# First stage of a one-core decoder step: the first conditioning result moved ahead of the weight roundings, low parts and scaled blocks moved behind pair 0, parameter transposes behind pair 1, and a pool that waits tile by tile

## Chip, cores and metric

The kernel runs on 1 core of one Trainium2 chip. The metric is device microseconds (us) of one execution. TensorE (PE) has two clock levels, 1.2 and 2.4 GHz; the profile writes the granted one as 0.5 or 1.0 of full speed.

## The reference

One inference step of a one-layer hybrid decoder: 512 prompt tokens and 8 sample tokens of width 1024, all float32. What matters for this change is the start of the layer:

```
cs = silu(c)                                  # c: 9 rows of 1024 (1 prompt, 8 samples)
mod = cs @ w_mod + b_mod                      # 1024 x 6144
sh1, sc1, g1, sh2, sc2, g2 = split(mod, 6)
h = rmsnorm(x, norm1_g) * (1 + sc1) + sh1     # 520 x 1024
u = h @ w_in                                  # 1024 x 8192: columns of q, f, i, gate, ...
f, k, q from sigmoids of u; HGRN2 recurrence with 8 heads; RG-LRU branch; merge; MLP
```

## The kernel before

Every large product is made three times on PE with rounded operands: a matrix is split into a high part (`whi`, `h_hi`, rounded by a ScalarE copy to the fp32r type) and a low part (`wlo`, `h_lo`, the difference, made by VectorE), and `products` adds high·high, high·low and low·high: 6 matmuls of 260 columns for one block of 128 rows of one weight tile. Activations lie transposed, as 8 blocks k of 128 features by 520 tokens.

The code is recorded in program order and a list scheduler places it on the engines; `behind(a, b)` is an ordering hint that forces a after b on an engine without a wait of its own. Each engine runs its list in order. SyncE (SP) issues nearly all loads.

The first stage (`begin`) does this. x is loaded, squared (ScalarE) for the norm, and transposed by PE into `self.x[k]` (tiles `ma`). `normed` broadcasts the factor of the norm and multiplies it into all 8 blocks on VectorE: u = x·rs, L477, tile `xn`. Meanwhile SP loads the conditioning weights `wm` (8 tiles of 1 MB, two for each pair of blocks: part 0 is the shift, part 1 the scale) and the first two tiles of w_in (`wst`, 0.5 MB each, the f and q columns of head 0), in the order wm, wm, wst, wm, wst, and then the other five wm. `first_w` splits these two (L1507 on ScalarE, L1508 on VectorE).

Then a loop runs over four pairs of blocks, k = 0, 2, 4, 6 (pairs 0 to 3 here):

- `mod(k)`: 16 matmuls of the program (32 in the trace) of `wm` against the conditioning rows (L382), and one ScalarE copy of the result out of PSUM (tile `modev`, L385);
- 6 matmuls (`products`) of the pair before;
- `mod_close`: four PE transposes of `modev` (L397), and on VectorE two reductions (L402), the bias (L405) and the gain (L409), which give scale and shift (`modT`);
- the other 18 matmuls of the pair before;
- `affine_split(k)`: h = u·scale + shift for the pair: high parts on ScalarE (L490, the samples' by L494), the full value on VectorE (L486 and L487 for samples, L495), the low part on VectorE (L496).

The products of pair 3 come last, and with them two PSUM accumulators (tile `mm`) are done: f and q of head 0. `parameters_in` transposes small parameters on PE (L242) and copies them out on VectorE (L243). Then the pool `start` is closed and the pool `hg` opened on its memory, and head 0 begins: three sigmoids on ScalarE (L157) read the two accumulators, and the next matmul group (the gate columns) needs the first accumulator's place. `head_sample` scales the sample states on ScalarE (L573) and adds to them on VectorE (L574), from `vb`, a broadcast that goes out to DRAM and back (L564, L566).

Of the kernel before, what the change touches and what calls it, by code (L numbers as in the profile page):

```python
# [6 lines left out]
F32 = mybir.dt.float32  # L7
# [9 lines left out]
L = 512  # L17
# [34 lines left out]
class Kernel:  # L52
# [321 lines left out]
    def mod(self, ws, ev, place):  # L374

        nc = self.nc
        ps = self.pps.tile([128, 512], F32, name="ps")
        for j, w in enumerate(ws):
            n = w.shape[2]
            for k in range(KO):  # L380
                r = 32 * (k % 4)
                ins = nc.tensor.matmul(ps[r:r + 32, j * n:j * n + n], self.cT[:, k, :], w[:, k, :], start=k < 4, stop=k >= KO - 4)  # L382
                if self.ppt_free:
                    self.turn = self.behind(ins, self.turn) if self.turn else ins
        ins = nc.scalar.copy(ev, ps)  # L385
        if self.ppt_free and self.last_hi:
            self.behind(ins, self.last_hi)
        self.mod_open = ev, place
# [76 lines left out]
    def normed(self):  # L465
# [9 lines left out]
        nc.vector.tensor_copy(rsb[:, L:], p2[:, :NB])  # L475
        for k in range(KO):
            nc.vector.tensor_tensor(self.u[:, k], self.x[k], rsb, OP.mult)  # L477

    def affine_split(self, k0):
# [6 lines left out]
        nc.vector.tensor_tensor(f[:, :, L:], u[:, ks, L:T], sc[:, :, 1:9], OP.mult)  # L486
        nc.vector.tensor_tensor(f[:, :, L:], f[:, :, L:], sh[:, :, 1:9], OP.add)  # L487
        for j in range(2):
# [4 lines left out]
            else:  # L493
                self.last_hi = self.behind(nc.scalar.copy(self.h_hi[:, ks, L:T], f[:, :, L:]), ins)  # L494
            nc.vector.tensor_scalar(f[:, j, :L], u[:, k, :L], sc[:, j, 0:1], sh[:, j, 0:1], OP.mult, OP.add)  # L495
            last = nc.vector.tensor_tensor(self.h_lo[:, k, :T], f[:, j], self.h_hi[:, k, :T].bitcast(F32), OP.subtract)  # L496
# [73 lines left out]
    def head_sample(self, h, st, vb, fkq, after):  # L570
        nc = self.nc
        for b in range(NB):
            nc.scalar.activation(st[:, b], st[:, b], AF.Copy, scale=fkq[:, 0, b:b + 1])  # L573
            after = self.behind(nc.vector.scalar_tensor_tensor(st[:, b], vb[:, b], fkq[:, 1, b:b + 1], st[:, b], OP.mult, OP.add), after)  # L574
# [11 lines left out]
    def head_prompt(self, h, f, X, q, v, og, st, vb, fkq):  # L586
# [5 lines left out]
        vn = self.slot(self.hg, "g")  # L592
        nc.scalar.copy(vn[:, :L], pv)

# [885 lines left out]

    def open_pool(self, name, bufs):
        self.scope = ExitStack()
        return self.scope.enter_context(self.tc.tile_pool(name=name, bufs=bufs))

# [3 lines left out]
    def begin(self):  # L1488
# [15 lines left out]

        def first_w(st):
            hi, lo = (self.start.tile([128, KO, 128], F32R, name=n, bufs=2) for n in ("whi", "wlo"))
            self.behind(nc.scalar.copy(hi, st), ready)  # L1507
            nc.vector.tensor_tensor(lo, st, hi.bitcast(F32), OP.subtract)  # L1508
            return hi, lo
# [18 lines left out]
        ready = nc.scalar.activation(self.act0, self.act0, AF.Sigmoid)  # L1528
        self.behind(self.behind(ready, squares), self.exps)
        first = [first_w(st) for st in staged]  # L1530
        par = self.parameters()
# [9 lines left out]
        for k in range(0, KO, 2):  # L1541
            mod(k)
            products(todo[:1])
            self.turn = self.mod_close(self.turn)
            products(todo[1:])
            self.split_last = self.affine_split(k)
            todo = [(j, k + n) for n in (0, 1) for j in (0, 1)]
        products(sorted(todo))
        self.parameters_in(*par)
        self.decays()  # L1550
        self.first = acc
        self.close_pool()
        self.hg = self.open_pool("hg", 2)
        self.ppt_free = False
# [62 lines left out]
```

## Time and profile before

| | |
|---|---|
| median of 3 runs | 1012.51 us (1012.02 to 1013.14) |
| the profiled execution's own time | 1012.61 us |
| its span (first to last instruction) | 1010.8 us |
| PE busy in the span | 981.9 us (97%) |
| VectorE (DVE) busy | 695.4 us (69%) |
| ScalarE (ACT) busy | 516.2 us (51%) |

The span is 1.8 us shorter than the time of the same execution, and that execution lies 0.1 us above the median. Busy time is an average over stages; what a change in one stage is worth is read from the waits of that stage.

### The profile page before, as it was taken

Reading aid. Unit: us, or ns where it says so; the run is one execution under the profiler, and the core shown is the slowest. Engines: PE = TensorE matmul, PEld = TensorE weight load, DVE = VectorE, ACT = ScalarE, POOL = GpSimd, SP = SyncE. Lnnn points to the kernel's source line nnn. Section 1 sums busy time; section 2 is a strip of 40 time slices with the busy share of each in tenths; the row PEclk is TensorE's granted clock in tenths of the full one; section 3 lists DMA queues with packets and bytes.
Section 4 is the critical chain, followed back from the end, with each engine's and each line's share of the span. In section 5 each row is a group of like instructions: output and inputs, shape, how many; then the busy total and the mean of one; then the engine's idle time right before and its main releaser. Section 6 shows DMA issues by size and latency. Waiting matters only on the chain.

```text
span 1010.8 us, 23254 instructions
## 1 busy us (share of the span) xinstructions
PE 981.9 (97%) x9585; PEld 955.3 (95%) x9585; DVE 695.4 (69%) x1543; ACT 516.2 (51%) x985; POOL 106.7 (11%) x193
## 2 busy tenths in 40 slices
PE   4999999999999999999999999999999999999995
PEld 3799999999999999999989999999999999999994
DVE  6768888698879868463233348767767766768775
ACT  5444763574575456351222234466556545646653
POOL 3000000000000000120000000022321331242040
PEclk9899999999999999999999999999999999999998
DMA  9794444353443434586566756222852582282242
GB/s 300 213 263 136 124 129 138 94 161 119 116 136 107 134 96 126 195 268 206 169 188 222 232 166 174 84 84 54 179 146 82 103 194 81 70 183 62 68 79 85
DMA packets 212572, 145.78 MB, mean 144 GB/s; under 512 B 6262, under 2 KB 196878, under 8 KB 212458
## 3 DMA queue, kind: packets, MB, share of 16 engines
q1 hardware_dynamic: 202562, 132.37, 44.1%
q0 software_dynamic: 9904, 11.92, 6.3%
q8 instruction: 75, 1.23, 0.5%
q14 instruction: 31, 0.25, 0.1%
HBM read 123.61 MB, written 13.39 MB: 136 GB/s over the span
## 4 chain that ended last, share of the span: by engine, by line
PE 90%; DVE 4%; DMA 3%; ACT 1%; issue 1%; SPq 0%; DVEq 0%; ACTq 0%; POOLq 0%
PE mm L118 65%; PE ps L1151 8%; PE pt L1151 4%; PE ps L382 2%; PE pb L1151 2%; PE pb L779 1%; PE ps L628 1%; DMA xn<-in_x_prompt_dram 1%; PE mm L1151 1%; PE pt L704 1%; PE pt L717 1%; DVE wlo L87 1%; DMA wst<-in_w_in_dram 1%; DMA vb<-vd 1%; PE pt L628 1%
## 5 line engine op out<-in xcount | busy, mean ns | idle before, releaser
L118 PE MATMUL mm<-h,whi 128*128 128x260 f32 (+1 forms) x3072 | 508.0, 285 | 1.9 <-ACT X L157 1.2
L118 PEld LDWEIGHTS mm<-h,whi 128*128 128x128 f32 x3072 | 425.9, 189 | 6.5 <-ACT whi L84 1.7
L118 PE MATMUL mm<-h,wlo 128*128 128x260 f32 (+1 forms) x1536 | 314.6, 284 | 0.0
L84 ACT CAST whi<-wst 128x1024 fp32r<-128x1024 f32 x166 | 173.9, 1050 | 208.8 <-PE mm L118 171.3
L87 DVE TENSOR_TENSOR wlo<-wst,whi 128x1024 fp32r<-128x1024 f32 x166 | 202.8, 1222 | 88.5 <-ACT whi L84 87.3
L118 PEld LDWEIGHTS mm<-h,wlo 128*128 128x128 f32 x1536 | 239.6, 189 | 0.1
L118 PE MATMUL mm<-a,whi 128*128 128x260 f32 x512 | 82.8, 283 | 0.0
L118 PEld LDWEIGHTS mm<-a,whi 128*128 128x128 f32 x512 | 70.3, 188 | 0.9 <-issue 0.8
L118 PE MATMUL mm<-a,wlo 128*128 128x260 f32 x256 | 51.7, 284 | 0.0
L1247 DVE TENSOR_TENSOR f<-f 128x260 f32<-128x260 f32 x64 | 27.3, 427 | 29.0 <-ACT f L1242 28.3
L880 POOL DMA_DIRECT2D t<-oaT_d x8 | 4.3, 551 | 375.8 <-PE mm L118 368.8
L1236 ACT ACTIVATE ft<-ft,fsh 128x512 f32<-128x512 f32 (+2 forms) x36 | 24.1, 676 | 35.9 <-DVE ft L1233 35.9
L118 PE MATMUL mm<-b,whi 128*128 128x260 f32 x256 | 41.6, 284 | 0.0
L1239 POOL TENSOR_TENSOR ft<-ft,fsh 128x8 f32<-128x8 f32 x28 | 18.5, 659 | 215.7 <-DVE ft L1233 215.7
L118 PEld LDWEIGHTS mm<-a,wlo 128*128 128x128 f32 x256 | 39.4, 188 | 0.0
L118 PEld LDWEIGHTS mm<-b,whi 128*128 128x128 f32 x256 | 35.0, 188 | 2.5 <-issue 2.5
L614 DVE TENSOR_TENSOR Y<-Y,tb 128x512 f32<-128x512 f32 x40 | 27.5, 688 | 11.0 <-ACT Y L616 5.5
L896 DVE TENSOR_TENSOR t<-mm,t 128x520 f32<-128x520 f32 x8 | 5.6, 699 | 37.0 <-PE mm L118 37.0
L1281 POOL DMA_DIRECT2D ma<-snap x28 | 26.1, 933 | 39.4 <-issue 22.1
L1263 POOL DMA_DIRECT2D ma<-snap x28 | 26.1, 932 | 39.7 <-DMA ma<-snap 23.2
L1242 ACT ACTIVATE f<-ft 128x520 f32<-128x520 f32 (+1 forms) x36 | 20.8, 589 | 14.9 <-POOL ft L1240 12.9
L573 ACT ACTIVATE st<-st,fkq 128x128 f32<-128x128 f32 x64 | 19.6, 390 | 13.9 <-DVE fkq L553 12.7
(488 smaller groups left out, 1816.6 us busy)
## 6 DMA issues: line engine op xcount, KB each, us to landing
wst<-in_w_in_dram SPq DMA_DIRECT2D x64, 512.0 KB
wm<-in_w_mod_dram SPq DMA_DIRECT2D x8, 2048.0 KB
wst<-in_w_ff_dram SPq DMA_DIRECT2D x64, 256.0 KB
wst<-in_w_ff_dram SPq DMA_DIRECT2D x32, 512.0 KB
wm<-in_w_mod_dram SPq DMA_DIRECT2D x8, 1024.0 KB
st<-in_state_hgrn_dram SPq DMA_DIRECT2D x8, 512.0 KB
vb<-vd SPq DMA_DIRECT2D x8, 512.0 KB
out_dram<-st SPq DMA_DIRECT2D x8, 512.0 KB
```

The lines of the kernel that those rows point to most:

```text
L84: ins = self.nc.scalar.copy(hi, st)
L87: ins = self.nc.vector.tensor_tensor(lo, st, hi.bitcast(F32), OP.subtract)
L118: self.last_product = self.nc.tensor.matmul(ps[:, s, :c.stop - c.start], x, y[:, c], start=first and n == 0, stop=last and n == 2)
L382: ins = nc.tensor.matmul(ps[r:r + 32, j * n:j * n + n], self.cT[:, k, :], w[:, k, :], start=k < 4, stop=k >= KO - 4)
L614: made = nc.vector.tensor_tensor(view(Y, b, 0, 2 * b, n, b), view(X, b, 0, 2 * b, n, b), fac, OP.mult)
L628: ins = nc.tensor.matmul(*args, start=True, stop=True)
L1151: ins = self.nc.tensor.matmul(ps, x[:, w], y[:, f], start=j in (1, 7, 2) and k == 0 and n == 0, stop=k == 3 and n == 2, skip_group_check=True)
L1236: nc.scalar.activation(t[:, :p], t[:, :p], AF.Relu, bias=sh[:, 0:1])
L1242: nc.scalar.activation(f, self.two(self.ft)[:, a:a + n], AF.Square)
L1247: self.nc.vector.tensor_tensor(f[:, n], f[:, a], f[:, b], op)
L1263: nc.gpsimd.dma_start(x[1][:, b], v[:, :n], accum_op=OP.add)
L1281: nc.gpsimd.dma_start(x[t][:, a], s[p], accum_op=OP.add)
```

## The change

Nothing is computed differently; instructions are put in another order, and waits are cut.

1. The copy of pair 0's conditioning result out of PSUM goes ahead of the two weight roundings (`first_w`) on ScalarE; the first rounding comes right behind it, the second behind pair 0's high parts.
2. On VectorE only the first two scaled blocks (`scaled(0)`, `scaled(1)`) come ahead of pair 0; the low parts of the two weights and blocks 2 and 3 come behind pair 0, blocks 4 to 7 behind pair 1.
3. In `affine_split` each full value (now L500) goes after the low part before it, so that the two blocks of a pair alternate.
4. `parameters_in` is called behind pair 1 instead of after the last products.
5. The pool `hg` is opened with `reuse_waits="tile"`: a tile in it waits for what lay in its own place, not for all of the closed pool.
6. ScalarE's scaling of the sample states is ordered behind the copy of the transposed values (`vcopy`).

```diff
--- before.py
+++ after.py
@@ -382,8 +382,8 @@
                 ins = nc.tensor.matmul(ps[r:r + 32, j * n:j * n + n], self.cT[:, k, :], w[:, k, :], start=k < 4, stop=k >= KO - 4)
                 if self.ppt_free:
                     self.turn = self.behind(ins, self.turn) if self.turn else ins
-        ins = nc.scalar.copy(ev, ps)
-        if self.ppt_free and self.last_hi:
+        self.evicted = ins = nc.scalar.copy(ev, ps)
+        if self.ppt_free:
             self.behind(ins, self.last_hi)
         self.mod_open = ev, place
 
@@ -473,8 +473,12 @@
         rsb = self.c128[:, :T]
         nc.scalar.copy(rsb[:, :L], ps)
         nc.vector.tensor_copy(rsb[:, L:], p2[:, :NB])
-        for k in range(KO):
-            nc.vector.tensor_tensor(self.u[:, k], self.x[k], rsb, OP.mult)
+
+        def scaled(k):
+            ins = nc.vector.tensor_tensor(self.u[:, k], self.x[k], rsb, OP.mult)
+            if self.split_last:
+                self.behind(ins, self.split_last)
+        self.scaled = scaled
 
     def affine_split(self, k0):
 
@@ -484,7 +488,8 @@
         sc, sh = (self.modT[:, p * 8 + k0:p * 8 + k0 + 2] for p in (1, 0))
         u = self.u
         nc.vector.tensor_tensor(f[:, :, L:], u[:, ks, L:T], sc[:, :, 1:9], OP.mult)
-        nc.vector.tensor_tensor(f[:, :, L:], f[:, :, L:], sh[:, :, 1:9], OP.add)
+        sample = nc.vector.tensor_tensor(f[:, :, L:], f[:, :, L:], sh[:, :, 1:9], OP.add)
+        last = None
         for j in range(2):
             k = k0 + j
             ins = nc.scalar.activation(self.h_hi[:, k, :L], u[:, k, :L], AF.Identity, bias=sh[:, j, 0:1], scale=sc[:, j, 0:1])
@@ -492,7 +497,8 @@
                 self.behind(ins, self.last_hi)
             else:
                 self.last_hi = self.behind(nc.scalar.copy(self.h_hi[:, ks, L:T], f[:, :, L:]), ins)
-            nc.vector.tensor_scalar(f[:, j, :L], u[:, k, :L], sc[:, j, 0:1], sh[:, j, 0:1], OP.mult, OP.add)
+            mid = nc.vector.tensor_scalar(f[:, j, :L], u[:, k, :L], sc[:, j, 0:1], sh[:, j, 0:1], OP.mult, OP.add)
+            self.behind(mid, last or sample)
             last = nc.vector.tensor_tensor(self.h_lo[:, k, :T], f[:, j], self.h_hi[:, k, :T].bitcast(F32), OP.subtract)
         self.last_hi = ins
         return last
@@ -570,7 +576,7 @@
     def head_sample(self, h, st, vb, fkq, after):
         nc = self.nc
         for b in range(NB):
-            nc.scalar.activation(st[:, b], st[:, b], AF.Copy, scale=fkq[:, 0, b:b + 1])
+            self.behind(nc.scalar.activation(st[:, b], st[:, b], AF.Copy, scale=fkq[:, 0, b:b + 1]), self.vcopy)
             after = self.behind(nc.vector.scalar_tensor_tensor(st[:, b], vb[:, b], fkq[:, 1, b:b + 1], st[:, b], OP.mult, OP.add), after)
         nc.sync.dma_start(self.o["hgrn_s"][0, :, h].rearrange("b k v -> k b v"), st)
         return after
@@ -590,7 +596,7 @@
         for c in range(NC):
             nc.tensor.transpose(pv[:, c * C:(c + 1) * C], v[:, c * C:(c + 1) * C], self.ident)
         vn = self.slot(self.hg, "g")
-        nc.scalar.copy(vn[:, :L], pv)
+        self.vcopy = nc.scalar.copy(vn[:, :L], pv)
 
 
 
@@ -1478,9 +1484,9 @@
         for _, fn, *a in steps:
             fn(*a)
 
-    def open_pool(self, name, bufs):
+    def open_pool(self, name, bufs, **kw):
         self.scope = ExitStack()
-        return self.scope.enter_context(self.tc.tile_pool(name=name, bufs=bufs))
+        return self.scope.enter_context(self.tc.tile_pool(name=name, bufs=bufs, **kw))
 
     def close_pool(self):
         self.scope.close()
@@ -1502,10 +1508,10 @@
         def mod(k):
             self.mod([raw.pop((part, k)) for part in (0, 1)], self.sm.tile([128, 512], F32, name="modev", bufs=1), (0, 2, k, 2))
 
-        def first_w(st):
+        def first_w(st, after):
             hi, lo = (self.start.tile([128, KO, 128], F32R, name=n, bufs=2) for n in ("whi", "wlo"))
-            self.behind(nc.scalar.copy(hi, st), ready)
-            nc.vector.tensor_tensor(lo, st, hi.bitcast(F32), OP.subtract)
+            self.behind(nc.scalar.copy(hi, st), after)
+            self.split_last = self.behind(nc.vector.tensor_tensor(lo, st, hi.bitcast(F32), OP.subtract), self.split_last)
             return hi, lo
 
         pm, pl = self.parameters_mod(), self.parameters_bounds()
@@ -1526,8 +1532,10 @@
         self.parameters_mod_in(pm)
         self.normed()
         ready = nc.scalar.activation(self.act0, self.act0, AF.Sigmoid)
-        self.behind(self.behind(ready, squares), self.exps)
-        first = [first_w(st) for st in staged]
+        self.last_hi = self.behind(self.behind(ready, squares), self.exps)
+        self.scaled(0)
+        self.scaled(1)
+        first = []
         par = self.parameters()
         acc = [self.pmm.tile([128, 2, 512], F32, name="mm") for _ in range(2)]
 
@@ -1544,13 +1552,20 @@
             self.turn = self.mod_close(self.turn)
             products(todo[1:])
             self.split_last = self.affine_split(k)
+            if k == 0:
+                first += first_w(staged[0], self.evicted), first_w(staged[1], self.last_hi)
+                for n in (2, 3):
+                    self.scaled(n)
+            if k == 2:
+                for n in range(4, KO):
+                    self.scaled(n)
+                self.parameters_in(*par)
             todo = [(j, k + n) for n in (0, 1) for j in (0, 1)]
         products(sorted(todo))
-        self.parameters_in(*par)
         self.decays()
         self.first = acc
         self.close_pool()
-        self.hg = self.open_pool("hg", 2)
+        self.hg = self.open_pool("hg", 2, reuse_waits="tile")
         self.ppt_free = False
         self.fkq = [self.hg.tile([128, 3, 32], F32, name=f"fkq{n}", bufs=1) for n in range(2)]
         for t in self.fkq:
```

The scheduler makes of it the following. On ScalarE, at the start of the loop (`whi` are the roundings of first_w, `modev` the conditioning result, `h` the high parts), before:

```order
L1528 ACTIVATE act0_103<-act0_103 1x1
L1507 CAST whi_340<-wst_187 128x1024
L1507 CAST whi_344<-wst_191 128x1024
L385 COPY modev_360<-ps_361 128x512
L490 ACTIVATE h_151<-xn_160,modT_182 128x512
L494 CAST h_151<-ht_388 128x2x8
L490 ACTIVATE h_151<-xn_160,modT_182 128x512
L385 COPY modev_398<-ps_399 128x512
```

and in the changed kernel:

```order
L1534 ACTIVATE act0_103<-act0_103 1x1
L385 COPY modev_346<-ps_347 128x512
L1513 CAST whi_384<-wst_187 128x1024
L495 ACTIVATE h_151<-xn_160,modT_182 128x512
L499 CAST h_151<-ht_374 128x2x8
L495 ACTIVATE h_151<-xn_160,modT_182 128x512
L1513 CAST whi_388<-wst_191 128x1024
L385 COPY modev_394<-ps_395 128x512
```

The first `modev` has moved ahead of both roundings, and the second rounding behind the high parts of pair 0.

On PE, between pair 0's last products and the products that follow the third conditioning matmuls, before:

```order
L118 MATMUL mm_359<-h_151,wlo_345 128x260 x2
L382 MATMUL ps_461<-wm_197,cT_176 32x256 [waits DMAHW6_49]
L382 MATMUL ps_461<-wm_197,cT_176 32x256 x7
L382 MATMUL ps_461<-wm_195,cT_176 32x256 [waits DMAHW5_49]
L382 MATMUL ps_461<-wm_195,cT_176 32x256 x7
L118 MATMUL mm_358<-h_151,whi_340 128x260 [waits Activation_49] x2
```

and now (`rb`, `rc`, `rd` are the rows of the small parameters; DMAHW and DMASW are semaphores of loads, and a name with _49 one of an engine):

```order
L118 MATMUL mm_345<-h_151,wlo_389 128x260 x2
L242 MATMUL ps_463<-ident_111,rb_334 128x57 [waits DMASW6_49,DMASW5_49,DMASW7_49,DMASW1_49,DMASW0_49]
L242 MATMUL ps_466<-ident_111,rc_335 128x64 [waits DMASW2_49,PE_49]
L242 MATMUL ps_469<-ident_111,rd_336 128x96 [waits DMASW3_49,DVE_49]
L242 MATMUL ps_472<-ident_111,rd_336 128x96 [waits DVE_49]
L382 MATMUL ps_476<-wm_197,cT_176 32x256 [waits DMAHW6_49,DVE_49]
L382 MATMUL ps_476<-wm_197,cT_176 32x256 x7
```

Four transposes stand ahead of pair 2's conditioning matmuls, which now wait for VectorE as well: these tiles `ps` share two PSUM places, so that the place of `ps_476` is free only after the copy out of `ps_469`.

On VectorE, from pair 1's reduction to pair 2's, before:

```order
L402 TENSOR_REDUCE modT_182<-pt_423 128x18 x2
L405 TENSOR_TENSOR modT_182<-modT_182,pm_316 128x2x18
L409 TENSOR_TENSOR modT_182<-modT_182,pm_316 128x18
L486 TENSOR_TENSOR ht_450<-xn_160,modT_182 128x2x8
L495 TENSOR_SCALAR ht_450<-xn_160,modT_182 128x512 x2
L487 TENSOR_TENSOR ht_450<-ht_450,modT_182 128x2x8
L496 TENSOR_TENSOR h_152<-ht_450,h_151 128x520 x2
L402 TENSOR_REDUCE modT_182<-pt_485 128x18 x2
```

and now, from the samples' part of pair 1 on:

```order
L490 TENSOR_TENSOR ht_446<-xn_160,modT_182 128x2x8
L243 COPY pa_460<-ps_463 128x57
L243 COPY pb_461<-ps_466 128x64
L491 TENSOR_TENSOR ht_446<-ht_446,modT_182 128x2x8
L500 TENSOR_SCALAR ht_446<-xn_160,modT_182 128x512
L243 COPY pc_462<-ps_469 128x96
L243 COPY pc_462<-ps_472 128x96
L502 TENSOR_TENSOR h_152<-ht_446,h_151 128x520
L500 TENSOR_SCALAR ht_446<-xn_160,modT_182 128x512
L502 TENSOR_TENSOR h_152<-ht_446,h_151 128x520
L478 TENSOR_TENSOR xn_160<-ma_231,c9_106 128x520
...
L402 TENSOR_REDUCE modT_182<-pt_500 128x18 x2
```

The four parameter copies stand inside pair 1's affine, and four scaled blocks (one shown) between it and pair 2's reduction.

On SP the load of the seventh w_in tile goes ahead of the eight stores of x (`xT_d`), where before it stood behind them.

## Rows read from the trace of the kernel before

**Rows 1.** What PE waited for over the whole span: total us, times, longest.
```profile
PE pt L397 <- ACT modev L385: 4.6, 1, 4.6
...
PE mm L118 <- ACT X L157: 1.2, 1, 1.2
...
PE mm L118 <- DVE h L496: 0.6, 1, 0.6
...
PE pb L779 <- ACT xcs L183: 0.5, 1, 0.5
```
**Rows 2.** Two stretches: engines' busy us, granted clock, DMA share, GB/s.
```profile
20.00:24.00 4.00, 1.44 (x28) 0.61 (x20) 4.00 (x9) 2.56 (x5) 0.00 (x0) 0.98 1.14 321
24.00:30.50 6.50, 4.08 (x33) 2.30 (x36) 6.18 (x18) 3.27 (x5) 0.00 (x0) 0.50 1.09 348
```
**Rows 3.** Timeline, 19 to 31 us: start, duration, instruction, idle before and its releaser.
```profile
19.50 1.93 PE L382 MATMUL ps<-wm,cT 128*32 128x256 f32 x32
...
19.79 0.16 DVE L475 COPY c<-ps 128x8 f32<-128x8 f32 x1
...
24.41 1.05 ACT L1507 CAST whi<-wst 128x1024 fp32r<-128x1024 f32 x1 [1.83 <-DMA wst<-in_w_in_dram]
...
25.36 0.58 ACT L385 COPY modev<-ps 128x512 f32<-128x512 f32 x1
...
25.99 1.11 PE L397 MATMUL pt<-ident,modev 128*128 128x128 f32 x4 [4.55 <-ACT modev L385]
...
27.53 3.46 PE L382 MATMUL ps<-wm,cT 128*32 128x256 f32 x32 [0.42 <-DVE wlo L1508]
```
**Rows 4.** SP's queue: one issue group of the conditioning weights.
```profile
17.72 12.88 SPq L371 DMA_DIRECT2D wm<-in_w_mod_dram  x5
```
**Rows 5.** Timeline of pair 1 and the start of pair 3, 32 to 40 us.
```profile
32.45 0.37 DVE L402 TENSOR_REDUCE modT<-pt 128x18 f32<-128x72 f32 x2 [1.37 <-PE pt L397]
...
33.30 0.82 ACT L490 ACTIVATE h<-xn,modT 128x512 fp32r<-128x512 f32 x1 [1.60 <-DVE modT L409]
...
34.49 1.93 PE L382 MATMUL ps<-wm,cT 128*32 128x256 f32 x32
...
34.50 0.21 ACT L494 CAST h<-ht 128x16 fp32r<-128x16 f32 x1 [0.39 <-DVE ht L487]
...
34.74 1.42 DVE L496 TENSOR_TENSOR h<-ht,h 128x520 fp32r<-128x520 f32 x2 [0.27 <-ACT h L494]
...
37.19 0.66 PE L397 MATMUL pt<-ident,modev 128*128 128x128 f32 x4
...
39.95 1.93 PE L382 MATMUL ps<-wm,cT 128*32 128x256 f32 x32
```
**Rows 6.** Groups of VectorE instructions, 0 to 52 us: count, busy us, mean ns.
```profile
L477 DVE TENSOR_TENSOR xn<-ma,c 128x520 f32<-128x520 f32 x8 | 5.0, 689 | 0.0
L495 DVE TENSOR_SCALAR ht<-xn,modT 128x512 f32<-128x512 f32 x8 | 4.0, 542 | 0.0
...
L1508 DVE TENSOR_TENSOR wlo<-wst,whi 128x1024 fp32r<-128x1024 f32 x2 | 2.4, 1221 | 0.0
```
**Rows 7.** Timeline, 46 to 52 us: parameter copies, last products, first sigmoids.
```profile
46.27 0.42 DVE L243 COPY pc<-ps 128x96 f32<-128x96 f32 x2 [0.21 <-PE ps L242]
...
47.35 0.51 PE L118 MATMUL mm<-h,whi 128*128 128x260 f32 x2 [0.62 <-DVE h L496]
...
50.33 0.60 ACT L157 ACTIVATE e<-mm 128x520 f32<-128x520 f32 x1 [1.44 <-PE mm L118]
...
51.48 0.74 PE L118 MATMUL mm<-h,whi 128*128 128x260 f32 x4 [1.24 <-ACT X L157]
```
**Rows 8.** Timeline of head 0, 67 to 77 us: a late weight, a broadcast.
```profile
67.89 1.05 ACT L84 CAST whi<-wst 128x1024 fp32r<-128x1024 f32 x1 [3.98 <-DMA wst<-in_w_in_dram]
...
70.70 1.25 SPq L566 DMA_DIRECT2D vb<-vd  x1
...
76.86 0.62 DVE L574 SCALAR_TENSOR_TENSOR st<-vb,fkq,st 128x128 f32<-128x128 f32 x2 [2.65 <-DMA vb<-vd]
```

## Prediction

> **What bounds the kernel now.** PE is busy 97% of the span, so time can only be won where PE waits. The list of PE's waits comes first: 4.6 us for the first conditioning result, 1.2 us for a sigmoid, 0.6 us for a low part, 0.5 us in head 0 [rows 1]. Everything but the last lies before 52 us, where this change works. Its ceiling is therefore a few microseconds of 1012.
>
> Next the timeline of the first wait [rows 3]. The conditioning matmuls of pair 0 (I call them mod 0, and so on) end at 19.50 + 1.93 = 21.43 us. Their copy out of PSUM starts at 25.36, because two roundings stand ahead of it on ScalarE, and the second began only at 24.41, when its weight landed. The transposes follow at 25.99, and mod 2 (pair 1) at 27.53.
>
> The reader should look closely at that 27.53. The row names a VectorE instruction as the releaser, but the PSUM place that mod 2 needs was last read by the copy at 19.79 [rows 3], long done. What is left of its waits is its weight. This can be checked: the w_in tile that was awaited landed at 24.41 at the latest, the next in SP's queue is the first of the last five conditioning weights [rows 4], 1.05 MB, and the stretch moved 348 GB/s with the DMA engines full [rows 2]: 24.4 + 3.0 = 27.4 us. So the loads, not the late copy, set the start of mod 2. By the same rate the pairs of weights for mod 4 and mod 6 are complete 6.0 us apart, at 33.4 and 39.4; they started at 34.49 and 39.95 [rows 5], so there PE was the later one, by 1.1 and 0.5 us.
>
> **The change, step by step.** Durations are those of the profiled execution.
>
> *First result ahead.* The copy can start at 21.7, the transposes at 22.3, and at the full-rate price of 0.66 us [rows 5] they end near 23.0 instead of 27.1. That is 4.1 us earlier for scale and shift. PE gains 0.1: its next instruction is mod 2, at 27.4 by the loads. The wait does not go away; it becomes a wait for a transfer.
>
> *The clock.* PE stood still for 4.55 us before [rows 3], and its clock was granted at 0.98 and then 0.50 (the lower level, 1.2 GHz) in the two stretches around it [rows 2]; mod 2 took 3.46 us where a full-rate one takes 1.93. Now PE stands still from 23.0 to 27.4, 4.4 us, nearly as long, so I take the same 3.46 us. No row shows this exact pattern, so it is bounded: if the clock stayed up, mod 2 would be 1.5 us shorter; if the half-rate time began with PE's stop, 1.5 us later than before, and ended as much later, 1.5 us of products would take double, costing 0.75.
>
> The Trainium skill, "TensorE: Matmul & The Clock Gate", in Part 1 on the clock gate, says that the gate's observation is free-running and not tied to the kernel's start, so that the point of change differs from run to run. By that rule the term could fall on either side in any one execution; a single profile, as here, cannot show it.
>
> *Low parts, scaled blocks, second rounding.* They move into 23 to 31 us, where PE waits and then runs mod 2. On VectorE pair 0's scale and shift are ready at 23.9 (0.85 us after the reduction starts, as 32.45 to 33.30 [rows 5]), its low parts at 26.8 (3.7 us after, as 32.45 to 36.16), two weight low parts of 1.22 us at 29.2, two scaled blocks of 0.65 us from start to start (5.0 us for eight) at 30.6 [rows 6]. Mod 2 ends at 30.9. So this costs nothing; without that cover it would cost up to 3.7 us.
>
> *Alternating order in the affine.* The first low part comes earlier by one 0.54 us operation [rows 6], the second at the same time: nothing on the path by itself.
>
> *Parameters behind pair 1.* Here the change adds a wait. Pair 0's products end at 34.4. Then four transposes, of which the third and fourth need VectorE to have copied out the first two. VectorE copies the first at 34.7 (0.2 us each, half of the 0.42 in [rows 7]), the second by 35.15; then in its queue stand a sample operation (0.2) and a full value (0.54), then the third copy, done at 36.0. Mod 4 needs that PSUM place: it starts at 36.05 instead of 34.49, 1.55 us later. In return the old place gives back its transposes and the 0.6 us wait near 47 us, both worked into the following.
>
> *Four scaled blocks behind pair 1.* Queued behind that third copy are the fourth, two low parts and a full value (38.05), and four scaled blocks at 0.65: 40.65. Pair 2's reduction stands behind them. Its transposes are done at 36.05 + 2.70 + 0.66 = 39.4 (37.19 − 34.49 = 2.70 [rows 5]), so it is 1.2 us late. Mod 6 runs at 36.05 + 5.46 = 41.5 (39.95 − 34.49 [rows 5]), its weight long there; pair 2's low parts are done at 40.65 + 3.7 = 44.35, just before their second use. Pair 3's reduction starts at 41.5 + 2.7 + 0.7 = 44.9, its low parts end at 47.8 and 48.6. PE arrives there at 41.5 + 5.46 = 46.95 and must wait for both. After the second, 16 matmuls remain at 0.12 us (18 and four transposes took 39.95 − 37.19 [rows 5]): 50.5, against 50.25 before. So up to here nothing is won: the 0.1 and the 0.6 us are spent.
>
> *Separate waits.* Before, the first sigmoid began at 50.33, with ScalarE idle for 1.44 us, and PE waited 1.24 us until 51.48 [rows 7]. The first accumulator was complete earlier, 12 matmuls or 1.45 us before the end, but the sigmoid's tile waited for all of the closed pool. Now it can begin when ScalarE is free and the accumulator done (49.1 to 49.5); two sigmoids of 0.5 to 0.6 us end at 50.6. The gate matmuls start at 50.65: **0.8 us** earlier than 51.48.
>
> *Later.* In head 0 a weight landed late (ScalarE idle 3.98 us), the broadcast was issued at 70.70 behind it, and VectorE waited 2.65 us for it [rows 8]; PE's 0.5 us [rows 1] follows from that chain. That weight's load now goes ahead of eight stores, so I take this **0.5 us** as won; bounds 0 and 0.5. Scaling the sample states later costs nothing while the broadcast lands after it: 2.5 us of room [rows 8]. Other stalls in the reordered heads can come or go; by the size of [rows 1], 0.5 us either way.
>
> Sum: 0.8 + 0.5 = 1.3 us. From the profiled 1012.6 that gives 1011.3, from the median of the runs shown 1012.5 − 1.3 = **1011.2 us**.
>
> **Rivals.** *(a) The clock stays up, or mod 2 is not held by its load: faster.* For it: the transposes are nearer to mod 0. Against it: the idle time is nearly unchanged. With mod 2 at 1.93 us all starts up to mod 6 move by 1.5 (34.5 and 40.0, still after their loads), 1012.5 − 2.8 = 1009.7. If mod 2 were free of its load, the next loads (33.4, 39.4) still hold: mod 6 at 39.4 instead of 41.5 gives 1009.1.
>
> *(b) It does nothing measurable.* The sigmoid's gain goes into waits for pair 3's low parts, and head 0 keeps its 0.5: 1012.0 to 1012.8. For it: PE's chain is already paced by loads and products.
>
> *(c) Slower: VectorE's queue.* The parameter copies and scaled blocks delay pair 2's reduction to 40.65. The slack behind it is 0.5 us; beyond, each microsecond passes to the end of pair 3. From a reduction at 42.0 on the stage is slower than before; at 43.5, were the copies and blocks as slow as twice their rows, the time would be 1014.0. Against it: these are durations of like instructions.
>
> **How the numbers follow.** Forecast 0.60, (a) 0.20, (b) 0.14, (c) 0.06. 0.2%, about what a measurement of this kernel can tell from no change, is 2.0 us: below 1010.5 is faster, above 1014.5 slower. (a) lies mostly beyond, and the forecast's edge adds a little: faster 0.20, same 0.77, slower 0.03. Range for 8 in 10: from between the two cases of (a), 1009.3, to 1013.0, which takes in (b) and the 0.75 us of the clock.
>
> **What would show it.** First `modev` copy near 21.7; PE idle to 27.4 and then released by a load (another name there is chance); half clock in mod 2; mod 4 at 36; a wait of PE for a low part near 47 to 49; first sigmoid near 49.5 and no wait of 1.2 us at 50; `vb` issued before 70. It is wrong if mod 2 starts well before 27, if it takes 1.9 us, or if mod 4 starts before 35.5.

## The result, and the profile after

The changed kernel took **1014.7 us** (median of 9 runs, 1013.62 to 1016.59) beside 1012.51 us for the kernel before, a ratio of 1.0021 with an interval of 1.0012 to 1.0030: it became slower by 0.2%, clear of the scatter. I had forecast 1011.2 us (1009.3 to 1013.0): the time lies outside the range, on the wrong side. The profiled execution (1015.5 us, 0.8 above the median) has a span of 1013.7 us, 2.9 more than before; the medians lie 2.2 us apart.

PE's waits of after, same view as [rows 1]: total us, times, longest.

```profile
PE ps L382 <- DMA wm<-in_w_mod_dram: 5.5, 1, 5.5
...
PE mm L118 <- DVE e L549: 1.8, 1, 1.8
PE pb L785 <- ACT xcs L183: 1.5, 1, 1.5
...
PE pt L710 <- ACT g L703: 0.8, 1, 0.8
```

The wait for the first conditioning result has become one for a load, as predicted, and the 1.2 us for a sigmoid is gone. But there are three waits behind 52 us, 4.1 us in all: for the product L549 of head 0's output gate (65 us), for `xcs` (88 us; the rounded input of the RG-LRU branch, whose products go to `pb`), and in the products of keys and values of the second head (L710, 140 us). Before there were 0.5 (`pb`, 85 us) and 0.4 (`pt`, 393 us).

PE in the first stage, timeline, to be read beside [rows 3, 5].

```profile
21.34 0.66 PE L397 MATMUL pt<-ident,modev 128*128 128x128 f32 x4 [0.72 <-ACT modev L385]
27.50 3.64 PE L382 MATMUL ps<-wm,cT 128*32 128x256 f32 x32 [5.50 <-DMA wm<-in_w_mod_dram]
31.07 1.24 PE L118 MATMUL mm<-h,whi 128*128 128x260 f32 x4
32.10 0.64 PE L118 MATMUL mm<-h,wlo 128*128 128x260 f32 x2
32.53 0.86 PE L397 MATMUL pt<-ident,modev 128*128 128x128 f32 x4
33.15 0.73 PE L118 MATMUL mm<-h,whi 128*128 128x260 f32 x4
...
36.90 1.93 PE L382 MATMUL ps<-wm,cT 128*32 128x256 f32 x32 [0.40 <-DVE pc L243]
```

Mod 2 is released by its load at 27.50. The half rate, over by mod 2's end before, now covers four products as well (1.24 us, then 0.73), the next two (0.64, elsewhere 0.40) and the transposes. The granted clock says the same; first after, then before (stretch, us, PE busy and count, clock, DMA share, GB/s).

```profile
24.00:27.00 3.00, 0.00 (x0) 0.87 1.09 348
...
30.50:34.00 3.50, 3.50 (x25) 0.63 1.09 347
```

```profile
24.00:27.00 3.00, 1.01 (x4) 0.50 1.09 349
...
30.50:34.00 3.50, 3.50 (x33) 0.98 1.09 347
```

The clock fell later in PE's idle time and rose later in the products: less of the half rate was spent idle.

The end of the stage and head 0, timeline of after (ScalarE, PE, VectorE; to be read beside [rows 7]).

```profile
50.38 0.61 ACT L157 ACTIVATE e<-mm 128x520 f32<-128x520 f32 x1 [0.29 <-ACT whi L84]
...
51.58 0.72 PE L118 MATMUL mm<-h,whi 128*128 128x260 f32 x4
...
60.13 0.30 ACT L770 CAST bdhlru_wa<-bdst 128x128 fp32r<-128x128 f32 x1 [4.10 <-DMA bdst<-in_lru_wa_dram]
...
62.03 0.61 ACT L157 ACTIVATE e<-mm 128x520 f32<-128x520 f32 x1
...
64.22 0.75 DVE L549 SCALAR_TENSOR_TENSOR e<-mm,pa,e 128x520 f32<-128x520 f32 x1
...
65.12 0.72 PE L118 MATMUL mm<-h,whi 128*128 128x260 f32 x4 [1.79 <-DVE e L549]
```

The gate matmuls start at 51.58 without a wait, against 51.48 [rows 7]: the stage has gained nothing. Then head 0 loses. Its output gate (sigmoid at 62.03, product L549 at 64.22) frees the accumulator that PE needs from 63.3 on. Ahead of that sigmoid in ScalarE's queue stand the roundings of the first block weights (`bdst`, the small matrices of the RG-LRU branch), and they waited 4.10 us for a load. In the kernel before the product ended just before PE came to it:

```profile
62.17 0.75 DVE L543 SCALAR_TENSOR_TENSOR e<-mm,pa,e 128x520 f32<-128x520 f32 x1
...
63.12 0.66 PE L118 MATMUL mm<-h,whi 128*128 128x260 f32 x4
```

The second loss, ScalarE and VectorE, 69 to 77 us, and PE at 88.

```profile
69.66 0.30 ACT L770 CAST bdhlru_wa<-bdst 128x128 fp32r<-128x128 f32 x1 [4.26 <-DMA bdst<-in_lru_wa_dram]
71.60 0.30 ACT L770 CAST bdhlru_wx<-bdst 128x128 fp32r<-128x128 f32 x1 [1.65 <-DMA bdst<-in_lru_wx_dram]
71.81 0.58 ACT L599 COPY g<-ps 128x512 f32<-128x512 f32 x1
72.29 2.45 ACT L579 ACTIVATE st<-st,fkq 128x128 f32<-128x128 f32 x8
74.64 1.04 ACT L84 CAST whi<-wst 128x1024 fp32r<-128x1024 f32 x1
...
75.71 1.23 DVE L87 TENSOR_TENSOR wlo<-wst,whi 128x1024 fp32r<-128x1024 f32 x1 [2.09 <-ACT whi L84]
...
87.93 0.39 PE L785 MATMUL pb<-xcs,bdhlru_wa 128*128 128x260 f32 x1 [1.49 <-ACT xcs L183]
```

The second block weights come late; behind them on ScalarE stands the value copy (L599), behind that, by the change's order, the state scaling (2.45 us), and behind that the rounding for which VectorE idles 2.09 us. Everything later in VectorE's queue slips, up to `xcs`. Before, the scaling lay in a wait of ScalarE long ahead of that, and the same rounding came at 70.79:

```profile
55.75 2.46 ACT L573 ACTIVATE st<-st,fkq 128x128 f32<-128x128 f32 x8 [1.19 <-DMA st<-in_state_hgrn_dram]
...
70.79 1.06 ACT L84 CAST whi<-wst 128x1024 fp32r<-128x1024 f32 x1 [0.96 <-PE mm L118]
```

Why the second block weights are late: SP's queue of after and then of before.

```profile
53.30 1.52 SPq L767 DMA_DIRECT2D bdst<-in_lru_wa_dram  x1
...
57.31 0.38 SPq L75 DMA_DIRECT2D wst<-in_w_in_dram  x1
57.74 6.79 SPq L545 DMA_DIRECT2D xT_d<-ma  x8
64.62 0.59 SPq L767 DMA_DIRECT2D bdst<-in_lru_wa_dram  x1
```

```profile
50.74 1.03 SPq L761 DMA_DIRECT2D bdst<-in_lru_wa_dram  x1
...
54.33 6.50 SPq L539 DMA_DIRECT2D xT_d<-ma  x8
61.23 0.38 SPq L75 DMA_DIRECT2D wst<-in_w_in_dram  x1
61.92 0.54 SPq L761 DMA_DIRECT2D bdst<-in_lru_wa_dram  x1
```

The seventh weight's load is not issued before 57.31, when VectorE has made the low part of the fifth weight, whose place it takes (57.29), the eight stores of x stand behind it, and the second block weights behind these: 64.62 instead of 61.92. The first block weight goes out 2.6 us later too, behind one weight more.

### The profile page after: what moved, and what is told of

Read it like the earlier page. It is cut to its first block, busy times and chain, and to the rows that moved or that the text cites. A ratio compares the mean times of both kernels' runs of the same rounds, so it can differ in the third digit from the quotient of the medians.

```text
span 1013.7 us, 23250 instructions
## 1 busy us (share of the span) xinstructions
PE 981.7 (97%) x9585; PEld 955.2 (94%) x9585; DVE 693.3 (68%) x1543; ACT 513.8 (51%) x985; POOL 106.7 (11%) x193
## 4 chain that ended last, share of the span: by engine, by line
PE 89%; DVE 3%; ACT 3%; DMA 2%; SPq 2%; issue 1%; DVEq 0%; ACTq 0%
PE mm L118 64%; PE ps L1157 8%; PE pt L1157 4%; PE ps L382 2%; PE pb L1157 2%; PE ps L634 1%; PE pb L785 1%; DMA wm<-in_w_mod_dram 1%; SPq L75 1%; PE mm L1157 1%; PE pt L710 1%; PE pt L723 1%; DMA bdst<-in_lru_wa_dram 1%; SPq L371 1%; DVE wlo L87 1%
## 5 line engine op out<-in xcount | busy, mean ns | idle before, releaser
L118 PEld LDWEIGHTS mm<-a,wlo 128*128 128x128 f32 x256 | 39.4, 188 | 0.0
L382 PE MATMUL ps<-wm,cT 128*32 128x256 f32 (+1 forms) x256 | 24.8, 522 | 5.9 <-DMA wm<-in_w_mod_dram 5.5
```

Source lines behind the costliest of these rows:

```text
L118: self.last_product = self.nc.tensor.matmul(ps[:, s, :c.stop - c.start], x, y[:, c], start=first and n == 0, stop=last and n == 2)
```

## The experiments

Ratios are to the kernel before on the same chip, with their 95% interval. The groups of runs were made on different chips, so between groups the ratios are compared and not the medians. The theories carry letters, and the expectations stand as they were written ahead of each run.

**One edit undone or done alone (four runs).** e1 and e2 differ from their parents in waits only; no engine's order moves.

```
e1: after;   open_pool("hg", 2, reuse_waits="tile")  ->  open_pool("hg", 2)
e2: before;  open_pool("hg", 2)  ->  open_pool("hg", 2, reuse_waits="tile")
e3: after;   self.parameters_in(*par) back behind products(sorted(todo))
e4: after;   behind(scaling of st, self.vcopy)  ->  scaling of st
```

> The changed kernel with one edit undone: the pool hg opens without separate waits, so each of its tiles waits for the whole closed pool again. No engine's order differs from the changed kernel, only waits. Theory A (the loss of 2.2 us is made in head 0 by the order of the program: loads of the block weights and stores of x stand elsewhere in the queue of loads, and the scaling of the sample states stands behind the value copy): the stalls of 1.8 us at 65 us and 1.5 us at 88 us stay, and the wait of 1.2 us before the first gate matmuls comes back in part: 1014.7 to 1016.0 us. Theory B (the separate waits themselves cause it: loads into hg start earlier and crowd the DMA engines before the block weights): both stalls shrink below 0.5 us, 1012.0 to 1013.0 us.

> The kernel before with the separate waits of hg alone; no engine's order differs from the kernel before. Theory A: no new stall in head 0; the first sigmoid starts about 0.8 us earlier and the 1.2 us wait of the first gate matmuls shrinks to 0.4 us or less: 1011.3 to 1012.3 us. Theory B: stalls in head 0 as in the changed kernel, 1013.5 to 1015 us.

> The changed kernel with the parameter transposes and copies put back after the last products; ScalarE and the queue of loads keep the changed kernel's order. Theory A: the third conditioning matmuls start about 0.9 us earlier (near 36.0 instead of 36.9), but the pair 3 waits and the place of the transposes give most of it back, and the head 0 stalls stay: 1014.2 to 1015.0 us. Theory C (the moved parameters hold the first stage and with it everything after): 1013.0 to 1013.8 us.

> The changed kernel without the ordering of the sample state scaling behind the value copy. Theory A, first form (this ordering makes the 1.5 us stall at 88 us, the queue of loads the 1.8 us one at 65 us): the scaling goes back into ScalarE's wait near 57 us, the stall at 88 goes and the one at 65 stays: 1013.0 to 1013.6 us. If the ordering makes both: 1011.5 to 1012.3 us. Theory D (the ordering costs nothing, as I predicted): 1014.4 to 1015.0 us.

| run | median us | ratio (interval) | PE's waits: sigmoid, output gate, `xcs` near 86 us |
|---|---|---|---|
| e1_pool | 1014.86 | 1.0021 (1.0012 to 1.0029) | 1.24, 0, 2.26 |
| e2_b_pool | 1013.48 | 1.0007 (0.9998 to 1.0015) | 0, 1.89, 0 |
| e3_params_back | 1014.23 | 1.0014 (1.0005 to 1.0022) | 0, 1.81, 1.46 |
| e4_no_vcopy | 1014.75 | 1.0013 (1.0005 to 1.0022) | 0, 2.09, 0 |

e2 shows the separate waits by themselves. In its timeline (ScalarE, VectorE, PE):

```profile
59.32 0.30 ACT L764 CAST bdhlru_wx<-bdst 128x128 fp32r<-128x128 f32 x1 [0.62 <-DMA bdst<-in_lru_wx_dram]
...
63.18 0.75 DVE L543 SCALAR_TENSOR_TENSOR e<-mm,pa,e 128x520 f32<-128x520 f32 x1
...
64.08 0.72 PE L118 MATMUL mm<-h,whi 128*128 128x260 f32 x4 [1.89 <-DVE e L543]
```

PE comes to this place 0.9 us earlier (62.19 instead of 63.12), the sigmoid's wait being gone; the gate's product starts 1.0 us later than before (62.17 there), behind block weights that were rounded 1.0 us later (59.32, 58.30 before); why their load was later is not shown. The gain of the first wait is lost in the second. e1 has the reverse: sigmoid's wait back, output gate's gone, same time. Both are misses of theory A, which had the stall at the output gate stay in e1 and no new stall in e2: this stall comes with the separate waits, in the old order and in the new. Theory B, for which both stalls come with them, has this one right and the one for `xcs` wrong: in e1 it grew to 2.26. e4 took away the waits for `xcs` (and the 0.8 us at L710, which comes and goes with it), but its runs fall into two groups, 1012.8 to 1013.6 (5) and 1014.7 to 1016.8 (7). The profiled one is of the upper, and its clock fell behind the output gate's wait of 2.09 us:

```profile
66.00:68.00 2.00, 2.00 (x12) 0.51 0.89 278
68.00:70.00 2.00, 2.00 (x13) 0.64 1.00 267
```

Four us at these rates lose some 1.7 us of work, about the distance of the groups. The other executions, which have no trace but a mean granted clock, bear this out: 0.993 or 0.994 in the five, 0.991 or 0.992 in the seven; 0.002 of 1013 us is 2 us, an estimate from rounded means. So theory A in its first form holds for the wait, while its time (1013.0 to 1013.6) holds for the lower group only; the median lies in the range of theory D, whose mechanism failed. e3 moved pair 2's conditioning by more than expected (7.61 us after mod 2's start instead of 9.40 in the changed kernel and 8.82 in e1) and left both stalls; its time lies where theory A had it.

**Parts combined (four runs).** e5 undoes the three edits together. e6 and e7 put the first block weights' roundings behind the output gate. e8 adds work: matmuls that nobody reads.

```
e5: after, with the edits of e1, e3 and e4
e6: before, with e2's edit, and for the first block weights (n == 0):
+   behind(rounding of bdst, sigmoid of og); behind(difference, product of og)
e7: after, with the edits of e3 and e4 and these two lines
e8: after;  behind mod_close of pair 0, 5 times:
+   nc.tensor.matmul(warm, self.ident, self.x[0][:, :512], start=True, stop=True)
```

> The changed kernel with three edits undone together: parameters back behind the last products, hg without separate waits, no ordering of the state scaling. What is left is the first result ahead, the low parts and scaled blocks behind pairs 0 and 1, and the alternating order. Theory E (the first stage gains what I worked out, less the clock; the loss is made in head 0 by the other edits): from the start of the conditioning matmuls of pair 1 to the gate matmuls 23.2 to 23.6 us (23.95 before) at equal clock, the sigmoid's wait of 1.2 us stays, no stall at 65 or 88 us: 1012.0 to 1013.0 us. Theory F (the new order of the loads in head 0, which this kernel keeps, makes the loss by itself): a stall of over 1 us at 65 or 88 us, 1013.8 us or more.

> The kernel before with the separate waits and one order more: the roundings of the first block weights (a ScalarE copy and a VectorE difference for each of two) go behind the output gate's sigmoid and product of head 0, which free the accumulator that TensorE waits for. Theory E (the gain of 1.1 us by the separate waits was lost because these roundings wait for a late load in front of the gate's product): the wait of 1.9 us at 62 us falls below 0.4 us, and the time is 1011.3 to 1012.0 us, below the kernel before. Rival G (the gate's product is late for its own inputs, or for the rounding of the next weight ahead of it): the wait stays above 1.2 us, 1013.0 us or more.

> The changed kernel with the parameters back behind the last products, no ordering of the state scaling, the separate waits kept, and the first block weights' roundings behind the output gate of head 0. Theory E: pair 1's conditioning to gate matmuls 22.2 to 22.9 us, no wait over 0.4 us at 60 to 66 us and none at 88 us: 1010.8 to 1011.8 us, the fastest of all so far. Rival G: 1013 us or more, with the stall at 62 us still there.

> The changed kernel with work added: five matmuls of 512 columns whose result nobody reads, on TensorE in its wait for the weight of pair 1 (22 to 27 us). The clock should then stay at the higher level: pair 1's conditioning matmuls near 1.93 us instead of 3.64, gate matmuls 1.5 to 2.5 us earlier than in the changed kernel. Theory H (what comes next is bound by loads, so time won before 52 us is given back at the output gate of head 0): that stall grows from 1.8 to 3.3 us or more, and the time is 1014.2 to 1015.0 us. Rival (TensorE's own work is the bound, a microsecond won stays won): the stall stays 1.8 us, 1012.3 to 1013.2 us.

| run | median us | ratio (interval) | PE's waits: sigmoid, output gate, `xcs` near 86 us |
|---|---|---|---|
| e5_first_only | 1011.93 | 0.9989 (0.9980 to 0.9998) | 1.24, 0, 0 |
| e6_b_pool_blocks | 1013.63 | 1.0006 (0.9997 to 1.0014) | 0, 0.76, 1.46 |
| e7_kept_parts | 1011.28 | 0.9986 (0.9977 to 0.9995) | 0, 0.50, 0 |
| e8_warm | 1013.43 | 1.0006 (0.9997 to 1.0015) | 0, 1.76, 1.44 |

e5 is faster than before: what is left of the change is good for 1.1 us, and theory F falls as stated (this kernel keeps the changed order of the loads and has no stall). Little of that lies in the stage: from mod 2 to the gate matmuls it took 24.01 us, or 23.6 less 0.4 of a longer half rate, which is the upper end of what I expected and 0.3 less than before. 0.5 is the `pb` wait of [rows 1], which is gone; the rest I cannot place. e7 has the lowest median of these, as theory E said, but is not clear of e5 (0.9986 and 0.9989); its stage, 23.27 us, and its wait at the gate, 0.50, are a little over what was expected (22.9 and 0.4). e6 is a miss: the wait at the gate fell from 1.89 to 0.76, not below 0.4, and where the kernel before waits 0.51 for `xcs` it waited 1.46; the time did not fall. The issue of the second block weight began at 62.73, behind the difference that frees its buffer and that I had moved back, and took 3.42 us instead of 0.54. That alone does not make the wait: the broadcast behind it in SP's queue went out at 70.98, only 0.3 us later than before, and the rounding of `xcs` started 0.4 us later (85.12, 84.76 before). The rest is that PE came 0.6 us earlier (84.35, 84.93 before): what it won ahead of `xcs` it gave back there.

In e8 mod 2 ran at the full rate, and theory H failed: the stage won 2.3 us (21.73 us from mod 2 to the gate matmuls, 24.08 in the changed kernel), the stall at the output gate stayed the same, and the ratio fell from 1.0021 to 1.0006, 1.5 us (the two intervals just overlap). The loads of head 0 had moved forward with the stage (the fifth weight issued at 48.25 instead of 50.73), so the chain from there to the gate moved as a whole.

**The loads' bound, and the two late edits (six runs).** The order behind the value copy in e9 and the five matmuls in e10 are put into e5, the matmuls into e7 (e11) and before (e12).

```
e9:  e5 without the edit of e4       e10: e5 with the matmuls of e8
e11: e7 with the matmuls of e8       e12: before, the matmuls ahead of mod_close of pair 0
e13: before with e2's edit and behind(scaling of st, self.vcopy)
e14: e5 without the edit of e1
```

> The kernel of the run e5_first_only with one edit of the change put back: the scaling of the sample states behind the copy of the transposed values. Theory E (this ordering costs TensorE a wait of its own near 85 to 88 us, whatever the other edits do): a wait of 1.4 us or more for xcs there and one of about 0.8 us near 140 us come back, 1013.6 to 1014.6 us. Rival (the ordering costs only together with the late loads that the separate waits make): no such wait, 1011.7 to 1012.3 us.

> The kernel of the run e5_first_only with work added: the five unread matmuls in TensorE's wait for pair 1's weight, to keep the clock up. Pair 1's conditioning matmuls take 1.93 us. Theory I (the weights of pairs 2 and 3, complete near 33.4 and 39.4 us by the rate of the loads, then hold TensorE, so that 2 us of clock are worth 0.5 us only): pair 2's conditioning starts at 33.2 us or later after a wait for its load, 1011.2 to 1011.7 us. Rival (these weights are there earlier, and the clock's 2 us are won whole): pair 2's conditioning at 32.6 us or earlier, 1009.7 to 1010.3 us.

> The kernel of the run e7_kept_parts with the same five unread matmuls added. Theory I: pair 3's conditioning starts at 39.4 us or later, and 0.5 to 1.2 us are won: 1010.2 to 1010.9 us. Rival (won whole): 1009.0 to 1009.6 us.

> The kernel before with the five unread matmuls added in its own wait, between pair 0's conditioning matmuls and the transposes of their result. Theory I: pair 0's transposes 0.66 us and pair 1's conditioning 1.93 us, a wait for the weights of pairs 2 and 3, and 0.3 to 0.8 us faster than the kernel before: 1012.1 to 1012.6 us beside its 1012.8 to 1013.0. Rival (won whole): 1.5 to 2 us faster, 1011.0 to 1011.4 us.

> The kernel before with the last two edits of the change alone: the separate waits of hg and the scaling of the sample states behind the value copy. The whole first stage is that of before. Theory E (these two make the loss): a wait of 1.5 to 2 us near 62 us at the output gate and one of 1.4 us or more near 86 us for xcs, 1014.5 to 1016.0 us. Rival (the loss needs the first stage's new order too): no wait at 86 us, 1013.0 to 1013.8 us.

> The kernel of the run e5_first_only with the separate waits of hg put back, without the later block weights of e7_kept_parts. Theory E (the separate waits give 1.2 us at the sigmoid and lose it at the output gate, whatever the first stage is): a wait of 1.6 to 2.2 us at 62 us, 1012.0 to 1013.0 us. Rival (the gain of e7_kept_parts came from the separate waits, and the order of the block weights did nothing): 1011.0 to 1011.6 us.

| run | median us | ratio (interval) | PE's waits: sigmoid, output gate, `xcs` near 86 us |
|---|---|---|---|
| e9_first_vcopy | 1016.12 | 1.0033 (1.0022 to 1.0045) | 1.24, 0, 2.26 |
| e10_first_warm | 1012.19 | 0.9999 (0.9990 to 1.0008) | 1.24, 0.22, 0 |
| e11_kept_warm | 1010.96 | 0.9986 (0.9977 to 0.9995) | 0, 1.09, 0 |
| e12_before_warm | 1012.32 | 1.0002 (0.9993 to 1.0011) | 1.24, 0.38, 0.19 |
| e13_two_late_edits | 1012.65 | 0.9999 (0.9990 to 1.0008) | 0, 1.70, 0.56 |
| e14_first_pool | 1012.78 | 0.9998 (0.9990 to 1.0007) | 0, 2.02, 0 |

In e10 the wait for the loads can be seen, timeline of PE:

```profile
27.44 1.93 PE L382 MATMUL ps<-wm,cT 128*32 128x256 f32 x32 [1.12 <-DMA wm<-in_w_mod_dram]
...
33.36 1.93 PE L382 MATMUL ps<-wm,cT 128*32 128x256 f32 x32 [0.42 <-DMA wm<-in_w_mod_dram]
...
39.40 1.93 PE L382 MATMUL ps<-wm,cT 128*32 128x256 f32 x32 [0.51 <-DMA wm<-in_w_mod_dram]
```

33.36 and 39.40: the loads' times of 33.4 and 39.4 that the prediction had worked out from their rate. Pair 3's conditioning can't start earlier, so a faster clock in mod 2 is worth little more than the half microsecond that PE was behind them: from mod 2 to the gate matmuls e10 took 23.30 us, e5 24.01. Nothing of it can be found in the time of e10 or e12, less than theory I had it. In e10's trace 0.22 at the output gate and a new wait of 0.80 at 436 us take it back; e12's is of its slowest execution (1014.15) and has a new wait of 1.92 for `xcs` at 260 us, so that it does not explain the median. e11 has the ratio of e7, its output gate's wait having grown from 0.50 to 1.09.

e9 shows what the order behind the value copy costs: from 0.9989 (e5) to 1.0033 (six executions), 4.5 us, more than theory E had. Its timeline (ScalarE, PE), and under it its window of 80 to 92 us with the granted clock:

```profile
70.64 0.30 ACT L770 CAST bdhlru_wx<-bdst 128x128 fp32r<-128x128 f32 x1 [1.67 <-DMA bdst<-in_lru_wx_dram]
70.85 0.58 ACT L599 COPY g<-ps 128x512 f32<-128x512 f32 x1
71.33 2.46 ACT L579 ACTIVATE st<-st,fkq 128x128 f32<-128x128 f32 x8
...
86.97 0.39 PE L785 MATMUL pb<-xcs,bdhlru_wa 128*128 128x260 f32 x1 [2.26 <-ACT xcs L183]
```

```profile
80.00:92.00 12.00, 9.74 (x165) 0.86 0.64 176
```

2.26 us of wait, 0.8 at L710, and 12 us at 0.86, some 1.7 us of work, make 4.7, about this distance. e13 is a second miss of theory E, and the most telling run: the same order in the kernel before costs nothing (0.9999; 1.0007 without it, in e2). Its timeline of ScalarE:

```profile
67.89 1.05 ACT L84 CAST whi<-wst 128x1024 fp32r<-128x1024 f32 x1 [5.75 <-DMA wst<-in_w_in_dram]
...
69.04 0.58 ACT L593 COPY g<-ps 128x512 f32<-128x512 f32 x1
69.52 2.45 ACT L573 ACTIVATE st<-st,fkq 128x128 f32<-128x128 f32 x8
71.88 0.28 ACT L764 CAST bdhlru_wx<-bdst 128x128 fp32r<-128x128 f32 x1
```

There the value copy comes at 69.04 and the rounding that is needed first at 67.89, ahead of it; the second of the block weights stands behind the scaling, where in e9 it stands ahead of the value copy and waits for its load. So the ordering by itself is not dear. That it becomes so where late block weights hold the value copy back, by the order of SP's queue, is argued from these timelines: no run moved those loads alone. e14 against e5 shows that the separate waits win nothing by themselves on the new first stage either (output gate 2.02 us, and a granted clock of 0.66 from 64 to 68). e14 against e7, which differ in the place of the block weights only, shows what that place does to the wait: 2.02 becomes 0.50. In time it is 1.2 us by the ratios, whose intervals overlap a little.

## Why the prediction was wrong

- **The first wait becomes a wait for a load:** right. Mod 2 was released at 27.50 (27.4 predicted), and the rate gave pairs 2 and 3 to 0.05 us in e10. The modev copy came at 20.73, not 21.7, because mod 0 started 0.8 us earlier in that execution (PE waited 3.5 us for x in all, 4.1 before; in e1 to e4 mod 0 came at 19.5 to 19.8); by the bound nothing hung on it.
- **The clock:** mis-sized. I had taken the same 3.46 us of half rate and no more, with +0.75 as upper bound; mod 2 took 3.64 and the four products, two products and transposes behind it 1.24, 0.64 and 0.86 us instead of 0.75, 0.40 and 0.66, together some 1.1 us. It was not this execution alone: with the new order pair 1's transposes started 4.40 to 5.04 us after mod 2 in eight profiled executions (the changed kernel, e1, e3, e4, e5, e7, e9, e14), with the old order 4.21 to 4.68 in four (before, e2, e6, e13), 5.03 and 4.22 in the two that are compared here, so that part of the difference is chance. The point at which it fell did scatter: from 24 to 27 us the granted clock was 0.87, 0.64, 0.68 and 0.56 in the changed kernel, e1, e3 and e5, whose programs agree up to mod 2. The Trainium skill, "TensorE: Matmul & The Clock Gate", Part 1, puts a scatter of the point of change at a kernel's start down to a free-running observation; the traces agree in the scatter, here of the point at which the clock falls, and cannot show its cause.
- **Parameters and scaled blocks:** right. Mod 4 followed mod 2 by 8.82 us in e1 and, with more of the half rate on products, 9.40 in the changed kernel (8.65 predicted), pair 2's reduction stood at 41.24 (40.65), PE waited for both low parts of pair 3 (0.20 and 0.28). Against e1, e3 shows the price of the moved parameters: 1.2 us at mod 4.
- **Separate waits, 0.8 us:** the gate matmuls did start without a wait, 24.08 us after mod 2; less the 1.1 us of clock, 23.0, as the sum had it (23.25). But the gain stops there. This is the first step that failed: I looked at who waited for the sigmoid, not at the next accumulator that PE needs, 12 us on. Its margin in the kernel before was 0.2 us (L543 ended at 62.92, PE came at 63.12).
- **"I take this 0.5 us as won" and "Scaling the sample states later costs nothing":** the second failed step, and the larger one. The 0.5 us by itself was there to be won: in e5 and e7, which keep the new order of the loads without the scaling's, PE does not wait for `xcs`. But the load that goes ahead of the stores is itself held back to 57.31 and holds up the stores and the block weights behind it; the broadcast `vb` was issued at 73.70, not before 70. And I priced the scaling by what consumes it, the broadcast, and not by what stands behind it in ScalarE's queue: 2.45 us ahead of a weight's rounding. In place of −0.5 there came +1.0 for `xcs` and +0.8 at L710; both are gone in e4, where the scaling alone is put back.
- **The sum:** stage +0.1 (−0.8 predicted), output gate +1.8, `xcs` +1.0, L710 +0.8, the old `pt` wait −0.4: 3.3, of the 2.9 by which the span grew; the difference of 0.4 I leave open.
- **The rivals:** (c) had the right sign and the wrong place; VectorE's queue in the stage held as worked out. (a)'s clock was tried by e8, which gained 1.5 us from a clock that stayed up, and by e10 and e12, which gained nothing measurable. My "0.5 us either way" for other stalls in the reordered heads should have been worked out from the order of the loads, which I had before me.

## What to carry to other kernels

A wait that is removed ahead of a chain of buffers is won only if the next holder of a buffer has margin: look for it one or two groups on, in the kernel before. When a load moves in an in-order queue, follow everything behind it to its consumers, and when work moves to a later place on an engine, price it by what stands behind it there. The kept parts, the first result ahead, the low parts behind pair 0 and separate waits, with the first block weights' roundings behind the output gate (e7), beat the kernel before by 1.4 us (0.9986, 0.9977 to 0.9995).

## What had not been expected of the hardware

A wait of TensorE can cost more than its length. Behind waits of 2.09 us (e4), 2.02 (e14) and 2.26 (e9) the granted clock fell for the next few us and some 1.7 us more were lost; behind 2.26 us in e1, and behind those of 1.70 to 1.89 in the changed kernel, e2, e3, e8 and e13, it stayed at 1.00 in the profiled execution. So the same stall can give two groups of times, as in e4. The mean clocks of the executions without a trace say that the shorter waits are not safe either: in e14 the three at 1013.8 us or more have 0.990 or 0.991, the others 0.993 or 0.994; in e13, profiled at 1.00 behind 1.70, the five at 1012.7 us or more all have 0.991, the others 0.992 to 0.994; and e2 has four of 11 at 0.990 or 0.991, the kernel before 4 of 117. Behind which stall the clock fell in them no trace shows.
